# The opening of a one-core hybrid decoder kernel: first tile in halves, norm row by matmul, split first weights, a shorter inverse square root

## The chip, the cores and the metric

The kernel runs on one core of a Trainium2 chip. The core has five engines that run side by side: TensorE (PE, matrix products; its weight loads are shown as PEld), VectorE (DVE), ScalarE (ACT), GpSimd (POOL) and SyncE (SP, which here only issues transfers). Transfers between device memory and on-chip memory are carried out by 16 DMA engines, fed by SP and POOL. The metric is the device time of one execution in microseconds (us).

## The reference

One step of a hybrid layer. All of it reads the same normalised input; for the change, the norms matter:

```python
def rmsnorm(x, g):
    xf = x.astype(jnp.float32)
    y = xf * lax.rsqrt(jnp.mean(xf * xf, axis=-1, keepdims=True) + EPS)
    return (y * g.astype(jnp.float32)).astype(x.dtype)

def hybrid_layer(x, ...):
    hn = rmsnorm(x, g_norm)
    u = hn @ w_in                      # (1024, 7176)
    xa, za, uq, uk, uv, uo, zb, ui, uf = jnp.split(u, SPLIT_IDX, axis=-1)
    yA, hA, bufA = rglru_branch(xa, ...)
    hB, C, n, m = mlstm_seq(q, k, v, ig, lf, C0, n0, m0)
    yB = sigmoid(uo) * hB
    yB = yB * lax.rsqrt(jnp.mean(yB * yB, axis=-1, keepdims=True) + EPS) * g_mhead
    merged = concat([yA * silu(za), yB * silu(zb)])
    return x + merged @ w_out, ...
```

It is computed for a prompt of 1024 tokens and for 8 single sample tokens (with their states), and a last `rmsnorm` is put on the sum. Everything is float32.

## The kernel before, in words

**Precision and tiling.** A float32 operand is split into a high part (`A.copy` into the type fp32r, on ACT, L70) and a low part (`V.tensor_tensor` subtract, on DVE, L71). A product is then three matmuls (`mm3`, L64 to L66: high by high, high by low, low by high). Tokens are tiled by 128 rows, eight tiles `x0` to `x7`, and tile 8 holds the 8 sample tokens. `w_in` is read in units of 512 columns in two row halves (`raw0`, `raw1`), each column part `a` of 256 by its own transfer (`load_raw`, L214).

**The opening** (L468 to L503). TensorE has nothing to multiply yet and runs 17 products of a tile of ones with itself into `pw` (L468, "warming"). Meanwhile SP issues, in this order: the first token tile `x4` (L365, 512 KB), the norm gain `g_norm` written into all 128 rows of `gn_b` (L470, 512 KB written from a 4 KB row), the first weights `raw0` part 0 (L214, 512 KB), the gate weights `wg` (L472, 32 KB), `raw1` part 0, the second token tile `x0`, and parts 1 of `raw0` and `raw1`.

For each tile, `x_stats` sums the squares (ACT, L370, with a read of the accumulator) and takes the inverse root of the mean (`rsqrt_mean`, L180, then `rsqrt`, L184 to L188). `x_turn` multiplies by that number and by `gn_b` (DVE, L381; the first tile in two halves), and transposes on TensorE (L385). `x_split` makes high and low parts of the transposed tile (`b12h`, `b12l`, `cb_hi`, `cb_lo`), while `w0_split` and `w1_split` do so for the weights (`wph`, `wpl`; `w1h`, `w1l`). `plain` multiplies the tile by the first two column blocks (`wph`, then `w1h`), 24 products each, and stores them. `x_combos` forms sums of blocks that later products use. Token tiles and weight splits share six buffers (`ws`, NWS = 6): four hold `w1h` and `w1l`, so two remain for tiles of x, and the fetch of the third tile waits until the first has been transposed.

**After the opening** the units of `w_in` follow one another in seven products each; gates, the recurrent scan, decode steps and the chunked mLSTM are woven between them; at the end the output projection runs tile by tile, each with a final norm (`finish`, L1233), and the last tile's norm (`last_tile`, L1335 to L1340) stands at the very end.

**`rsqrt`** (L183 to L188) is called for the nine tiles of x, for each of the eight chunks of heads (`m_n`, four columns), once for the decode heads (32 columns), for the eight results of `finish` and in `last_tile`. It takes a root on ACT, a reciprocal on DVE, and one Newton step of three DVE instructions.

**What sets the order.** Each engine runs its own instructions in a fixed order. That order isn't the program's order throughout: the framework plans ahead from its own estimates of when data arrive and places an instruction where its inputs are expected. SP carries out its issues in order; an issue that waits for a buffer holds those behind it.

Of the kernel before, what the change touches and what calls it, by code (L numbers as in the profile page):

```python
# [9 lines left out]
F32 = mybir.dt.float32  # L10
F32R = mybir.dt.float32r
BF16 = mybir.dt.bfloat16
AF = mybir.ActivationFunctionType
ALU = mybir.AluOpType
# [3 lines left out]
P = 128  # L18
T = 1024
HT = 512  # L20
# [5 lines left out]
EPS = 1e-6  # L26
# [23 lines left out]
def hymba_kernel(  # L50
# [7 lines left out]
    V, A, G, TE = nc.vector, nc.scalar, nc.gpsimd, nc.tensor  # L58
    ld = nc.sync.dma_start
    stq = nc.gpsimd.dma_start  # L60

    def mm3(out, ah, al, bh, bl, first, last):

        TE.matmul(out, ah, bh, start=first, stop=False, skip_group_check=True)  # L64
        TE.matmul(out, ah, bl, start=False, stop=False, skip_group_check=True)  # L65
        TE.matmul(out, al, bh, start=False, stop=last, skip_group_check=True)  # L66
# [12 lines left out]
    def ps(tag, shape):  # L79
        return psp.tile(shape, F32, tag=tag, name=f"ps_{tag}", bufs=NBUF.get(tag, 1))  # L80
# [6 lines left out]
    rawp = ctx.enter_context(tc.tile_pool(name="rawp", bufs=1))  # L87
# [6 lines left out]
    def ws(shape, name, dt=F32R):  # L94

        return wsp.tile(shape, dt, tag="ws", name=name)

    def sg(shape, name, dt=F32):

        return stg.tile(shape, dt, tag="stg", name=name)  # L100
# [4 lines left out]
    def dconst(shape, name):  # L105

        return dpool.tile(shape, F32, tag=name, name=name)
# [4 lines left out]
    ones = dconst([P, P], "ones")  # L112
# [34 lines left out]
    st0 = dconst([P, 9, 3], "st0")  # L147
# [29 lines left out]

    def rsqrt_mean(out, v, t, n):

        V.tensor_scalar(v, v, 1.0 / n, EPS, op0=ALU.mult, op1=ALU.add)  # L180
        rsqrt(out, v, t)

    def rsqrt(out, v, t):  # L183
        A.activation(out, v, AF.Sqrt)  # L184
        V.reciprocal(out, out)
        V.tensor_tensor(t, out, out, op=ALU.mult)
        V.scalar_tensor_tensor(t, t, -0.5, v, op0=ALU.mult, op1=ALU.mult)
        V.scalar_tensor_tensor(out, t, 1.5, out, op0=ALU.add, op1=ALU.mult)  # L188

    cb = [(big(2 * q, [P, 4, HT], f"cb_hi{q}"), big(2 * q + 1, [P, 4, HT], f"cb_lo{q}")) for q in range(7)]  # L190

# [9 lines left out]
    COL = {"q": C_Q, "k": C_K, "v": C_V, "o": C_O, "z": C_ZB, "x": C_XA, "y": C_ZA}  # L201
    units = [((c[0], int(c[1])), (c[2], int(c[3]))) for c in UNITS]
    raws = {}

    def load_raw(u, b, parts=(0, 1)):

        if u >= len(units):
            return
        if (u, b) not in raws:
            raws[u, b] = rawp.tile([P, 4, 512], F32, tag=f"raw{b}", name=f"raw{b}_{u}")  # L210
        for a in parts:
            kind, j = units[u][a]
            c = COL[kind] + j * 256
            ld(raws[u, b][:, :, a * 256:(a + 1) * 256],  # L214
               w_in[0, b * HT:(b + 1) * HT, c:c + 256].rearrange("(k p) c -> p k c", p=P))
# [141 lines left out]
    fp = es_f.enter_context(tc.tile_pool(name="f_start", bufs=1))  # L357
    gn_b = fp.tile([P, T], F32, tag="gn_b", name="gn_b")
    xorder = [4, 0, 8, 5, 1, 6, 2, 7, 3]
    rows_of = lambda i: P if i < 8 else NB  # L360
    xt, xps, bf = {}, {}, {}

    def x_fetch(i):
        xt[i] = ws([P, T], f"x{i}", F32)
        ld(xt[i][:rows_of(i)], x_prompt[0, i * P:(i + 1) * P, :] if i < 8 else x_sample[:, 0, :])  # L365

    def x_stats(i):
        n = rows_of(i)
        junk = fp.tile([P, T], BF16, tag="junk", name="junk")
        A.activation(junk[:n], xt[i][:n], AF.Square, accum_out=st0[:n, i, 0:1])  # L370
        rsqrt_mean(st0[:n, i, 1:2], st0[:n, i, 0:1], st0[:n, i, 2:3], T)
# [92 lines left out]

    pw = ps("tr", [P, P])

    for _ in range(17):
        TE.matmul(pw, ones, ones, start=True, stop=True)  # L468
    x_fetch(xorder[0])
    ld(gn_b, g_norm[0].partition_broadcast(P))  # L470
    load_raw(0, 0, (0,))
    ld(wg, w_in[0, :, C_G:C_G + 8].rearrange("(k p) c -> p k c", p=P))  # L472
    load_raw(0, 1, (0,))
    x_fetch(xorder[1])
# [1 line left out]
    load_raw(0, 1, (1,))  # L476
    ld(bgate[:, 0:4], b_mi[0].partition_broadcast(P))
    ld(bgate[:, 4:8], b_mf[0].partition_broadcast(P))
    x_stats(xorder[0])
    x_stats(xorder[1])  # L480
    for m, i in enumerate(xorder):
        x_turn(m)
# [37 lines left out]
    fp = es_f.enter_context(tc.tile_pool(name="f_gates", bufs=1, reuse_waits="tile"))  # L520
# [414 lines left out]
    def decode_outputs():  # L935
# [36 lines left out]
        yield  # L972
        V.tensor_tensor(rsd, v4(tmp, 0), v4(tmp, 1), op=ALU.add)
        rsqrt_mean(rsq, rsd, rst, 4 * 256)
        V.tensor_tensor(num, num, dz, op=ALU.mult)
        V.tensor_tensor(num, num, gm4.unsqueeze(2).to_broadcast([P, 8, NB]), op=ALU.mult)
# [180 lines left out]
    def m_n(c):  # L1157

        m = ch[c]["m"]
        dn, ss, t, rs, u = (m[:, n] for n in range(5))  # L1160
        V.scalar_tensor_tensor(t, dn, -1.0, em_t[:, c, :], op0=ALU.mult, op1=ALU.max)
        V.tensor_tensor(t, t, dn, op=ALU.max)
        V.scalar_tensor_tensor(t, t, EPS, t, op0=ALU.mult, op1=ALU.mult)
        V.scalar_tensor_tensor(t, ss, 1.0 / (4 * 256), t, op0=ALU.mult, op1=ALU.add)
        rsqrt(rs, t, u)
        ch[c]["mh"], ch[c]["ml"] = ws([P, 8, P], f"mh{c}"), ws([P, 8, P], f"ml{c}")

# [64 lines left out]

    def finish(n, yt, ms, dst, later=False):  # L1233

        V.tensor_scalar(ms[:n, 0:1], ms[:n, 0:1], ms[:n, 1:2], 1.0 / T, op0=ALU.add, op1=ALU.mult)
        V.tensor_scalar(ms[:n, 0:1], ms[:n, 0:1], EPS, None, op0=ALU.add)
        rsqrt(ms[:n, 2:3], ms[:n, 0:1], ms[:n, 3:4])

        def out():
            for half in range(2):  # L1240
                hs = slice(half * HT, (half + 1) * HT)
                V.scalar_tensor_tensor(yt[half][:n], yt[half][:n], ms[:n, 2:3], mx["gf"][half][:n], op0=ALU.mult, op1=ALU.mult)
                stq(dst[:, hs], yt[half][:n])
        if later:
            tails.append(out)
        else:
            out()

    def dec_end():

        z = sg([P, HT], "zd")
        A.copy(z, dec_o[0])
        yd = [sg([32, HT], f"yd{half}") for half in range(2)]
        for half in range(2):
            stq(yd[half][0:NB], x_sample[:, 0, half * HT:(half + 1) * HT])
        yield
        ms = fms()
        for half in range(2):
            pd = ps("tr", [32, HT])
            TE.matmul(pd, sel[:, half, :], z, start=True, stop=True)  # L1260
            V.tensor_tensor(yd[half][0:NB], yd[half][0:NB], pd[0:NB], op=ALU.add)
            A.activation(pd[0:NB], yd[half][0:NB], AF.Square, accum_out=ms[0:NB, half:half + 1])
            yield
        finish(NB, yd, ms, y_s[:, 0, :])
# [50 lines left out]
    def last_tile():  # L1315
        x = ot[NCH - 1]
        ms = mx["p2"].tile([P, 6], F32, tag="ms7", name="ms7")
        y = [sg([P, HT], f"y{n}") for n in range(2)]
        yg = [sg([P, HT], f"yg{n}") for n in range(2)]
        for n in range(2):  # L1320
            stq(y[n], x_prompt[0, (NCH - 1) * P:T, n * HT:(n + 1) * HT])
        mh, ml = ch[NCH - 1]["mh"], ch[NCH - 1]["ml"]
        for i, cs in enumerate(LP):
            for k in range(8):
                w = wo[8 + k]
                mm3(x["p", i], mh[:, k, :], ml[:, k, :], w[:, 0, cs], w[:, 1, cs], False, k == 7)
            v = (y[0], y[1][:, 0:256], y[1][:, 256:512])[i]
            vg = (yg[0], yg[1][:, 0:256], yg[1][:, 256:512])[i]
            gv = (mx["gf"][0], mx["gf"][1][:, 0:256], mx["gf"][1][:, 256:512])[i]
            V.tensor_tensor(v, v, x["p", i], op=ALU.add)  # L1330
            A.activation(x["p", i], v, AF.Square, accum_out=ms[:, i:i + 1])
            V.tensor_tensor(vg, v, gv, op=ALU.mult)
            if i == 1:
                V.tensor_scalar(ms[:, 0:1], ms[:, 0:1], ms[:, 1:2], T * EPS, op0=ALU.add, op1=ALU.add)
        V.tensor_scalar(ms[:, 0:1], ms[:, 0:1], ms[:, 2:3], 1.0 / T, op0=ALU.add, op1=ALU.mult)  # L1335
        rsqrt(ms[:, 4:5], ms[:, 0:1], ms[:, 5:6])
        V.tensor_scalar(yg[0], yg[0], ms[:, 4:5], None, op0=ALU.mult)
        A.mul(yg[1], yg[1], ms[:, 4:5])
        for n in range(2):
            ld(y_p[0, (NCH - 1) * P:T, n * HT:(n + 1) * HT], yg[n])  # L1340
# [92 lines left out]
    for n in range(4, N):  # L1433
        c, h = n // 4, n % 4
# [8 lines left out]
        if h == 2 or n == 4:  # L1443
            z_load(c if h == 2 else 0)
        if h == 0:
            m_n(c - 1)
            fill(2)
            m_k(n + 1)
# [38 lines left out]
    while work:  # L1487
        fill(1)
    tail()
    last_tile()  # L1490
    es_m.close()

# [32 lines left out]
```

## Time and profile before

| what | value |
|---|---|
| runs (us) | 957.59, 960.5, 959.0; median 959.0 |
| the profiled execution's own time | 958.7 us |
| its span, first to last instruction | 956.9 us |
| mean granted TensorE clock | 0.997 of full speed |
| DVE, ACT, POOL busy | 75%, 61%, 15% of the span |

The profile gives times from the start of the span. "Idle before" an instruction is the time for which its engine had nothing to do, with what ended it. The chain that ended last is followed back from the last instruction: at each step to what released it. "PEclk" is the TensorE clock that was granted, as a share of full speed.

### The profile page before, as it was taken

How to read it: one execution, taken by the hardware profiler on the slowest of the kernel's cores; microseconds unless marked ns; L12 is line 12 of the kernel's file. 1: busy time of each engine (PE TensorE's matmuls, PEld its weight loads, DVE VectorE, ACT ScalarE, POOL GpSimd, SP SyncE). 2: the span in 40 equal slices, each digit the busy share in tenths (PEclk: the TensorE clock that was granted, in tenths of full speed). 3: DMA queues.
4: the chain of work that ended last, by engine and by line, in shares of the span. 5: the costliest groups of instructions: out<-in, count | busy, mean ns of one | idle time of the engine just before them, and what ended most of it. 6: DMA issues, size and time to landing. Idle time of an engine off the chain costs nothing.

```text
span 956.9 us, 15419 instructions
## 1 busy us (share of the span) xinstructions
PE 930.1 (97%) x5370; PEld 761.9 (80%) x5370; DVE 713.1 (75%) x1482; ACT 586.9 (61%) x1048; POOL 146.2 (15%) x259
## 2 busy tenths in 40 slices
PE   7999999999999999999899999999989999999997
PEld 7887767777787987777689898876667888888886
DVE  5876798879898878989687867686556676676664
ACT  5654447768677757677568774465546466455633
POOL 1111112112212122111211221010200100000020
PEclk9999999999999999999999999999999999999999
DMA  5441447356745465465537362434873763564361
GB/s 185 146 127 43 132 125 266 107 183 192 255 146 201 157 205 174 160 205 205 178 134 221 122 210 88 156 113 147 297 222 97 190 185 104 156 183 133 114 115 46
DMA packets 131363, 153.71 MB, mean 161 GB/s; under 512 B 15798, under 2 KB 110038, under 8 KB 131278
## 3 DMA queue, kind: packets, MB, share of 16 engines
q1 hardware_dynamic: 113558, 96.86, 34.5%
q0 software_dynamic: 17728, 55.87, 16.3%
q8 instruction: 42, 0.69, 0.3%
q14 instruction: 35, 0.29, 0.1%
HBM read 101.11 MB, written 51.65 MB: 160 GB/s over the span
## 4 chain that ended last, share of the span: by engine, by line
PE 71%; DVE 10%; DMA 8%; issue 5%; ACT 4%; SPq 1%; POOL 0%; DVEq 0%; ACTq 0%; POOLq 0%
PE ps_o L66 12%; PE ps_o L64 11%; PE ps_o L65 11%; PE ps_kv L64 8%; PE ps_kv L66 8%; PE ps_kv L65 8%; PE ps_tr L227 2%; DMA W<-d_alpha 2%; DMA Cb<-in_state_mlstm_C_dram 2%; PE ps_s L1075 1%; DMA out_dram<-Cb 1%; DVE wl L71 1%; DMA x<-in_x_prompt_dram 1%; PE ps_qp L64 1%; PE ps_tr L1211 1%
## 5 line engine op out<-in xcount | busy, mean ns | idle before, releaser
L64 PE MATMUL ps_kv<-cb_hi,wh 128*128 128x512 f32 x320 | 128.2, 401 | 3.5 <-ACT s L308 3.5
L71 DVE TENSOR_TENSOR wl<-raw,wh 128x1024 fp32r<-128x1024 f32 x91 | 111.2, 1222 | 27.2 <-ACT wh L70 16.8
L70 ACT CAST wh<-raw 128x1024 fp32r<-128x1024 f32 x91 | 95.4, 1048 | 58.3 <-PE ps_o L65 23.8
L66 PE MATMUL ps_kv<-cb_hi,wl 128*128 128x512 f32 x320 | 125.7, 393 | 0.0
L65 PE MATMUL ps_kv<-cb_lo,wh 128*128 128x512 f32 x320 | 125.2, 391 | 0.0
L64 PE MATMUL ps_o<-cb_hi,wh 128*128 128x512 f32 x240 | 95.0, 396 | 0.0
L66 PE MATMUL ps_o<-cb_hi,wl 128*128 128x512 f32 x240 | 94.1, 392 | 0.0
L65 PE MATMUL ps_o<-cb_lo,wh 128*128 128x512 f32 x240 | 93.5, 390 | 0.0
L64 PEld LDWEIGHTS ps_kv<-cb_hi,wh 128*128 128x128 f32 x320 | 60.1, 188 | 26.8 <-ACT s L308 4.5
L66 PEld LDWEIGHTS ps_kv<-cb_hi,wl 128*128 128x128 f32 x320 | 60.1, 188 | 15.6 <-issue 2.5
L65 PEld LDWEIGHTS ps_kv<-cb_lo,wh 128*128 128x128 f32 x320 | 60.2, 188 | 12.5 <-issue 0.8
L64 PE MATMUL ps_kv<-wh,cb_hi 128*128 128x256 f32 x192 | 55.4, 288 | 0.0
L65 PE MATMUL ps_kv<-wl,cb_hi 128*128 128x256 f32 x192 | 54.3, 283 | 0.0
L66 PE MATMUL ps_kv<-wh,cb_lo 128*128 128x256 f32 x192 | 54.3, 283 | 0.0
L64 PEld LDWEIGHTS ps_o<-cb_hi,wh 128*128 128x128 f32 x240 | 45.1, 188 | 10.7 <-issue 1.7
L66 PEld LDWEIGHTS ps_o<-cb_hi,wl 128*128 128x128 f32 x240 | 45.0, 188 | 10.6 <-issue 0.8
L64 PE MATMUL ps_o<-wo,rh 128*128 128x512 f32 (+1 forms) x136 | 53.4, 393 | 0.0
L66 PE MATMUL ps_o<-wo,ml 128*128 128x512 f32 (+1 forms) x136 | 52.1, 383 | 0.8 <-DVE ml L71 0.8
L64 PE MATMUL ps_o<-wo,mh 128*128 128x512 f32 (+1 forms) x136 | 52.8, 388 | 0.0
L65 PEld LDWEIGHTS ps_o<-cb_lo,wh 128*128 128x128 f32 x240 | 45.1, 188 | 9.2
L66 PE MATMUL ps_o<-wo,rl 128*128 128x512 f32 (+1 forms) x136 | 51.8, 381 | 0.0
L65 PE MATMUL ps_o<-wo,rh 128*128 128x512 f32 (+1 forms) x136 | 51.8, 381 | 0.0
(475 smaller groups left out, 2540.2 us busy)
## 6 DMA issues: line engine op xcount, KB each, us to landing
raw<-in_w_in_dram SPq DMA_DIRECT2D x56, 512.0 KB
Cb<-in_state_mlstm_C_dram SPq DMA_DIRECT2D x32, 256.0 KB
out_dram<-Cb POOLq DMA_DIRECT2D x32, 256.0 KB, 4.5
qk<-d_qk SPq DMA_DIRECT2D x32, 256.0 KB
oraw<-in_w_out_dram SPq DMA_DIRECT2D x16, 512.0 KB
d_qk<-s POOLq DMA_DIRECT2D x24, 256.0 KB, 4.4
x<-in_x_prompt_dram SPq DMA_DIRECT2D x8, 512.0 KB
d_x<-s POOLq DMA_DIRECT2D x16, 256.0 KB, 2.7
```

What stands on the lines that cost most here:

```text
L64: TE.matmul(out, ah, bh, start=first, stop=False, skip_group_check=True)
L65: TE.matmul(out, ah, bl, start=False, stop=False, skip_group_check=True)
L66: TE.matmul(out, al, bh, start=False, stop=last, skip_group_check=True)
L70: A.copy(hi, src)
L71: V.tensor_tensor(lo, src, hi.bitcast(F32), op=ALU.subtract)
L227: TE.matmul(pz[32 * g:32 * g + 32, :], hnd[:, k, :], raws[u, k // 4][:, k % 4, :], start=k < 4, stop=k >= 4, skip_group_check=True)
L1075: TE.matmul(S, qk[:, 2 + kb, :], qk[:, kb, :], start=kb == 0, stop=kb == 1)
L1211: TE.matmul(dec_o[0][32 * g:32 * g + 32, :], md, oraw[m][:, half * 512:(half + 1) * 512], start=n == 0, stop=n == 14, skip_group_check=True)
```

## The change

Four edits. In the opening, `x4` comes in two column halves of 256 KB, each squared and summed when it is there, and the two sums are combined on DVE (`x_first`, `x_first_stats`). `gn_b` isn't written by a transfer any more: two transfers of 2 KB bring the two halves of the row (`grow`), and two products of a column of ones with the row (one row deep, 512 columns) spread each over 128 rows in PSUM, which ACT copies to `gn_b`. They stand among the warming products, of which 6 + 3 remain out of 17. The first weights `raw0` part 0 come in two transfers of 256 KB. And `rsqrt` is written anew: with the mean scaled by a quarter, it is root, reciprocal, one step (multiply and add) and reciprocal where the operand is one column; for more columns that step takes two instructions.

```diff
     def rsqrt_mean(out, v, t, n):
-        V.tensor_scalar(v, v, 1.0 / n, EPS, op0=ALU.mult, op1=ALU.add)
+        V.tensor_scalar(v, v, 0.25 / n, 0.25 * EPS, op0=ALU.mult, op1=ALU.add)
         rsqrt(out, v, t)
     def rsqrt(out, v, t):
         A.activation(out, v, AF.Sqrt)
-        V.reciprocal(out, out)
-        V.tensor_tensor(t, out, out, op=ALU.mult)
-        V.scalar_tensor_tensor(t, t, -0.5, v, op0=ALU.mult, op1=ALU.mult)
-        V.scalar_tensor_tensor(out, t, 1.5, out, op0=ALU.add, op1=ALU.mult)
+        V.reciprocal(t, out)
+        if len(v.shape) == 2 and v.shape[1] == 1:
+            V.scalar_tensor_tensor(t, v, t, out, op0=ALU.mult, op1=ALU.add)
+        else:
+            V.tensor_tensor(t, t, v, op=ALU.mult)
+            V.tensor_tensor(t, t, out, op=ALU.add)
+        V.reciprocal(out, t)
...
+    def x_first():
+        i = xorder[0]
+        xt[i] = ws([P, T], f"x{i}", F32)
+        for half in range(2):
+            hs = slice(half * HT, (half + 1) * HT)
+            ld(xt[i][:, hs], x_prompt[0, i * P:(i + 1) * P, hs])
+
+    def x_first_stats():
+        i = xorder[0]
+        junk = fp.tile([P, T], BF16, tag="junk", name="junk")
+        sq = fp.tile([P, 2], F32, tag="sq", name="sq")
+        for half in range(2):
+            hs = slice(half * HT, (half + 1) * HT)
+            A.activation(junk[:, hs], xt[i][:, hs], AF.Square, accum_out=sq[:, half:half + 1])
+        v = st0[:, i, 0:1]
+        V.tensor_scalar(sq[:, 0:1], sq[:, 0:1], 0.25 / T, 0.25 * EPS, op0=ALU.mult, op1=ALU.add)
+        V.scalar_tensor_tensor(v, sq[:, 1:2], 0.25 / T, sq[:, 0:1], op0=ALU.mult, op1=ALU.add)
+        rsqrt(st0[:, i, 1:2], v, st0[:, i, 2:3])
...
     pw = ps("tr", [P, P])
-    for _ in range(17):
+    x_first()
+    grow = [sg([1, HT], f"grow{half}") for half in range(2)]
+    for half in range(2):
+        ld(grow[half], g_norm[:, half * HT:(half + 1) * HT])
+    raws[0, 0] = rawp.tile([P, 4, 512], F32, tag="raw0", name="raw0_0")
+    kind, j = units[0][0]
+    c0 = COL[kind] + j * 256
+    for k in (0, 2):
+        ld(raws[0, 0][:, k:k + 2, 0:256], w_in[0, k * P:(k + 2) * P, c0:c0 + 256].rearrange("(k p) c -> p k c", p=P))
+
+    for _ in range(6):
         TE.matmul(pw, ones, ones, start=True, stop=True)
-    x_fetch(xorder[0])
-    ld(gn_b, g_norm[0].partition_broadcast(P))
-    load_raw(0, 0, (0,))
+    for half in range(2):
+        pb = ps("o", [P, 512])
+        TE.matmul(pb, ones[0:1, :], grow[half], start=True, stop=True)
+        A.copy(gn_b[:, half * HT:(half + 1) * HT], pb)
+    for _ in range(3):
+        TE.matmul(pw, ones, ones, start=True, stop=True)
     ld(wg, w_in[0, :, C_G:C_G + 8].rearrange("(k p) c -> p k c", p=P))
...
-    x_stats(xorder[0])
+    x_first_stats()
     x_stats(xorder[1])
```

In `m_n`, `finish` and `last_tile` the constants in front of `rsqrt` are multiplied by 0.25, with the same instructions.

More of the change, by code (lines that the diff above doesn't have):

```diff
@@ L1162, in m_n @@
         V.tensor_tensor(t, t, dn, op=ALU.max)
-        V.scalar_tensor_tensor(t, t, EPS, t, op0=ALU.mult, op1=ALU.mult)
-        V.scalar_tensor_tensor(t, ss, 1.0 / (4 * 256), t, op0=ALU.mult, op1=ALU.add)
+        V.scalar_tensor_tensor(t, t, 0.25 * EPS, t, op0=ALU.mult, op1=ALU.mult)
+        V.scalar_tensor_tensor(t, ss, 0.25 / (4 * 256), t, op0=ALU.mult, op1=ALU.add)
         rsqrt(rs, t, u)
@@ L1233, in finish @@
     def finish(n, yt, ms, dst, later=False):
-        V.tensor_scalar(ms[:n, 0:1], ms[:n, 0:1], ms[:n, 1:2], 1.0 / T, op0=ALU.add, op1=ALU.mult)
-        V.tensor_scalar(ms[:n, 0:1], ms[:n, 0:1], EPS, None, op0=ALU.add)
+        V.tensor_scalar(ms[:n, 0:1], ms[:n, 0:1], ms[:n, 1:2], 0.25 / T, op0=ALU.add, op1=ALU.mult)
+        V.tensor_scalar(ms[:n, 0:1], ms[:n, 0:1], 0.25 * EPS, None, op0=ALU.add)
         rsqrt(ms[:n, 2:3], ms[:n, 0:1], ms[:n, 3:4])
@@ L1334, in last_tile @@
                 V.tensor_scalar(ms[:, 0:1], ms[:, 0:1], ms[:, 1:2], T * EPS, op0=ALU.add, op1=ALU.add)
-        V.tensor_scalar(ms[:, 0:1], ms[:, 0:1], ms[:, 2:3], 1.0 / T, op0=ALU.add, op1=ALU.mult)
+        V.tensor_scalar(ms[:, 0:1], ms[:, 0:1], ms[:, 2:3], 0.25 / T, op0=ALU.add, op1=ALU.mult)
         rsqrt(ms[:, 4:5], ms[:, 0:1], ms[:, 5:6])
```

## The prediction

> **What bounds the kernel now.** I read the page's span, shares and chain first.
>
> ```profile
> span 956.9 us, 15419 instructions
> PE 930.1 (97%) x5370; PEld 761.9 (80%) x5370; DVE 713.1 (75%) x1482; ACT 586.9 (61%) x1048; POOL 146.2 (15%) x259
> PE 71%; DVE 10%; DMA 8%; issue 5%; ACT 4%; SPq 1%; POOL 0%; DVEq 0%; ACTq 0%; POOLq 0%
> ```
>
> TensorE is busy all but 27 us, and the change touches none of its products after the opening. So only two things can be gained: an earlier start of the chain, and steps shorter where the chain runs over a norm. A start that comes earlier should pass on nearly whole, since everything later hangs on what came before and nothing is tied to an absolute time.
>
> So the timeline of the opening comes next.
>
> ```profile
> 1.14 6.53 PE L468 MATMUL ps_tr<-ones 128*128 128x128 f32 x34 [1.14 <-POOL ones L113]
> 4.53 1.06 ACT L370 ACTIVATE junk<-x 128x1024 bf16<-128x1024 f32 x1 [2.29 <-DMA x<-in_x_prompt_dram]
> 5.49 0.19 ACT L370 ACTIVATION_READ_ACCUMULATOR junk<-x 128x1 f32 x1
> 5.71 0.15 DVE L180 TENSOR_SCALAR st<-st 128x1 f32<-128x1 f32 x1 [5.71 <-ACT junk L370]
> 6.72 0.16 DVE L188 SCALAR_TENSOR_TENSOR st<-st 128x1 f32<-128x1 f32 x1
> 6.91 1.41 DVE L381 SCALAR_TENSOR_TENSOR x<-x,st,gn_b 128x512 f32<-128x512 f32 x2
> 7.76 1.27 PE L385 MATMUL ps_kv<-idF,x 128*128 128x128 f32 x8
> 8.05 0.62 ACT L70 CAST wph<-raw 128x512 fp32r<-128x512 f32 x1 [1.95 <-DMA raw<-in_w_in_dram]
> 8.57 0.24 ACT L70 CAST wph<-wg 128x64 fp32r<-128x64 f32 x1
> 8.72 0.61 ACT L70 CAST wph<-raw 128x512 fp32r<-128x512 f32 x1
> 9.24 0.57 ACT L70 CAST b12h<-ps_kv 128x512 fp32r<-128x512 f32 x1
> 10.92 0.39 PE L66 MATMUL ps_o<-wph,b12l 128*128 128x264 f32 x1 [0.55 <-DVE b12l L71]
> 11.23 0.59 ACT L407 COPY b12f<-ps_kv 128x512 f32<-128x512 f32 x1
> 14.53 1.07 ACT L70 CAST w1h<-raw 128x1024 fp32r<-128x1024 f32 x1
> 15.74 0.39 PE L65 MATMUL ps_o<-w1l,b12h 128*128 128x256 f32 x1 [0.92 <-DVE w1l L71]
> 17.48 1.28 DVE L381 SCALAR_TENSOR_TENSOR x<-x,st,gn_b 128x1024 f32<-128x1024 f32 x1
> 20.09 0.60 PE L385 MATMUL ps_s<-idF,x 128*128 128x128 f32 x4
> ```
>
> Two paths meet at the first useful product. Path one: `x4` lands (4.53), square, norm, scaling (6.91), transposes (7.76). Path two: the weights land only at 8.05; three casts then stand ahead of `b12h` on ACT, which starts at 9.24 though its first four transposes were through about 8.3. From 8.05 to the end of the cast at 15.6 ACT isn't idle at all. The chain agrees that the weights' transfer is the first long piece:
>
> ```profile
> 1.66 6.37 DMA raw<-in_w_in_dram
> 8.05 1.28 ACT wph L70 x3
> 21.16 3.89 DMA x<-in_x_prompt_dram
> 53.87 0.17 DVE st L186
> 54.07 0.17 DVE st L187
> 63.00 0.17 DVE st L188
> 952.29 0.17 DVE ms L187
> 952.48 0.17 DVE ms L188
> 952.68 0.72 ACT yg L1338
> ```
>
> It then runs over the second tile's transposes (20.09), the fetch of the next tile (21.16), and, further on, norms at 53.87, 63.0 and 952.3.
>
> **Part one: the norm row off the transfers.** It removes 512 KB that stand between `x4` and the first weights.
>
> ```profile
> 3.00:5.00 2.00, 2.00 (x11) 2.00 (x11) 0.00 (x0) 0.47 (x1) 0.00 (x0) 1.00 1.00 346
> 9.11 0.35 SPq L365 DMA_DIRECT2D x<-in_x_sample_dram  x1
> 1.66 0.43 SPq L214 DMA_DIRECT2D raw<-in_w_in_dram  x1
> ```
>
> The DMA engines are full, at 346 GB/s, so 524 kB are 1.5 us. The first weights would land at 8.05 - 1.5 = 6.5, and their first half another 262 / 346 = 0.76 us sooner, at 5.8. SP issues three transfers more in front of what follows (one half of x, one row half, one half of the weights: two of 0.43 and one of 0.35, 1.2 us). The weights' first issue moves from 1.66 to about 2.5, behind two issues of x and two of the row. I cost that at nothing: the 512 KB of x alone occupy the DMA engines until nearly 4, so the queue doesn't run empty. If it did, the loss would be at most that 0.8 us. The bounds for this part are -2.3 (the first half) and -0.7 (1.5 less 0.8) on the landing; for the later weights I take -1.5.
>
> Splitting x into halves is free by the same row: transfers behind each other overlap. A rule speaks against it. The Trainium skill, "DMA: Bandwidth & Descriptors", section "Bandwidth", asks for transfers of 1 MiB or more, because each carries a fixed cost of about 2 us. Paid in series it would put the second half of x 2 us later and my sum at about 959; the full DMA engines above say that it is overlapped.
>
> **Part two: the norm row by products.** It adds two products of 512 columns in float32, two copies on ACT, and removes eight warming products. A float32 matmul shows as two passes.
>
> ```profile
> 4.07 0.85 PE L468 MATMUL ps_tr<-ones 128*128 128x128 f32 x3
> 32.00 1.05 PE L227 MATMUL ps_tr<-raw,hnd 128*32 128x512 f32 x2
> ```
>
> Three passes of 128 columns start within 0.85 less the last one's 0.42, so 0.21 each; a product of 512 columns is 2 x 4 x 0.21 = 1.7 us at that early rate, and 1.05 us later, at full rate, by the row of 32.00. Six warming products end at 1.14 + 12 x 0.21 = 3.7. The row itself stands behind x in the queue; I let it land with x, at 4.5 (bounds: 3.7, when TensorE is free; 5.8, with the weights behind it). Product one then ends at 6.2, its copy (0.59, as the copy at 11.23) about 6.9. Product two ends at 7.3 at full rate or 7.9 at the early one, its copy at 7.9 or 8.5. The two copies fall where ACT is idle today (the 1.95 us ahead of 8.05); without that cover they cost 1.2.
>
> **Part three: halves of x and the shorter norm on path one.** The first half is squared while the second is under way, so after 4.53 only 512 columns are left: half of 1.06, saving about 0.5. `rsqrt` loses one DVE step of 0.2 (the spacing of 6.72 to 6.91). The factor would be ready at 6.91 - 0.5 - 0.2 = 6.2. But the scaling now waits for `gn_b`: first half at 6.9, exactly today's start; second half at 7.9 instead of 7.6. So path one gains nothing and its second half loses 0.3.
>
> **Part four: the meeting point.** With weights at 5.8 and 6.5, the three casts (8.05 to 9.24, 1.2 us) and the two copies fit on ACT between 5.8 and 8.2. `b12h` then starts when its transposes are through, 8.2 to 8.3, instead of 9.24: 1.0 us gained. After that ACT has the same 6.3 us of work in front of it as today, and the later weights come 1.5 us sooner, so the 1.0 us holds to `w1h` (14.53), the products at 15.74, the second tile's scaling and the fetch at 21.16. Bounds: the row late (5.8) puts scaling at 8.2 and `b12h` at 9.5, a loss of 0.3; the row early and the weights' whole 1.5 us bring -1.5.
>
> **Part five: the norms elsewhere.** One step of 0.2 falls away on the chain at 53.87 to 54.07 and at 63.0; in most other tiles it lies between splits that fill DVE. I take 0.4 (bounds 0.2 and 0.8: one tile pays, or four). At the very end nothing covers it: 0.2. In `m_n` and the decode heads the number of instructions is the same, four on DVE; cost nothing. The extra SP issues later: none.
>
> Sum: -1.0 - 0.4 - 0.2 = -1.6 us. The profiled execution took 958.7 us, 0.3 below the median of the three runs; 958.7 - 1.6 = **957.1 us**.
>
> **Rivals.**
>
> *The slow stretch goes too.* Windows of TensorE's clock:
>
> ```profile
> 9.76:13.17 3.41, 2.76 (x20) 2.55 (x21) 3.06 (x7) 3.41 (x8) 0.00 (x0) 1.00 1.06 346
> 13.17:16.58 3.41, 1.90 (x14) 1.50 (x13) 3.13 (x8) 2.95 (x6) 0.58 (x1) 1.00 0.22 60
> 16.58:20.00 3.42, 3.42 (x19) 3.42 (x18) 2.18 (x3) 0.00 (x0) 0.00 (x0) 0.50 0.02 5
> ```
>
> After a stretch with TensorE busy only 1.90 of 3.41 us the granted clock is 0.50 for 3.4 us. Were the products of `w1` at full rate, the second tile's transposes would start when its scaling ends, 17.48 + 1.28 = 18.8, not 20.09: another 1.2 us, 955.9. For it: 1.0 us earlier, more of the products at 15.74 fall into the window before 16.58. Against: the gap between the two blocks of products is the same length, since `w1h` moves with `wph`. The Trainium skill, "TensorE: Matmul & The Clock Gate", section "What's actually happening", says that this window runs freely and isn't tied to the kernel's start; by that rule the gap can fall across two windows in one execution and into one in another, before and after alike. The page's one execution can't show that.
>
> *The weights' lead is idle.* If `gn_b`'s second half and the DVE work behind it (scaling until 8.6, then the weights' low parts) hold `b12l` until today's time, the opening gains nothing: only the norms, -0.6, 958.1. For: the low part starts the stalled product at 10.92, not the high one. Against: the low parts of the weights can go before the scaling.
>
> *Slower: the copies stand ahead of the squares on ACT.* ACT runs in a planned order. If both copies are placed before the squares, they end at 7.9, the squares with their read at 9.1 instead of 5.7, 3.4 later; less 0.2 for the step, the scaling starts at 10.1 and `b12h` about 11.4, 2.2 later than 9.24. Norms give back 0.6: +1.6, 960.3. It decides from the point at which the planner expects the row before the second half of x. Against: the row is issued behind both halves.
>
> *The planned order differs further on.* If one fetch of a tile of x slips by a turn, it costs such a wait as the 3.89 at 21.16: 958.7 + 3.9 - 0.6 for the norms = 962.0. Nothing in the profile speaks for it.
>
> **How the numbers follow.** Forecast 0.38, slow stretch gone 0.28, lead idle 0.15, copies first 0.12, order 0.07. A measurement of this kernel tells a change from none at about 0.3%, 2.9 us: below 956.1 or above 961.9. Below lie 0.24 of the slow-stretch case and 0.15 of the forecast's (where the start gains 1.5 and the norms 0.8, 956.2 or less): 0.39. Above lie 0.03 of the copies-first case (row at 5.8, 1.3 later, and the second product at the early rate, 0.6 more: 962.2) and the order case: 0.10. Range: low 957.1 - 1.2 (slow stretch) - 0.9 (better bounds) = 955.0; high 960.3, the copies-first case.
>
> **What would show it.** Right: the first cast of weights near 5.8, `b12h` starting near 8.2, the first stalled product a microsecond before 10.92, the fetch of the third long tile near 20, three DVE steps after each root, and the last root's steps 0.2 shorter. Wrong: weights still landing near 8 (then the issue on SP held them); squares behind the copies; scaling well after 6.9; a clock of 1.00 throughout the opening would mean the second case. A difference after 70 us larger than at 21 would mean that the planned order changed.

## The result, and the profile after

The changed kernel is slower. Over 22 runs of each its median is 960.95 us against 956.76 us. The ratio is estimated as 1.0039 with a 95% interval of 1.0027 to 1.0051 (the quotient of the two medians alone is 1.0044): some 3.7 us lost where 1.6 us were forecast as gained.

The profiled execution of the changed kernel took 958.68 us. It is one of its quicker ones, 2.3 us under its median, so its page looks much like the page of before: the same span, TensorE as busy, and a chain with somewhat more of TensorE in it (79% against 71%). These are its span, its shares of busy time and the first line of its chain of waits.

```profile
span 956.9 us, 15387 instructions
PE 930.8 (97%) x5358; PEld 762.2 (80%) x5358; DVE 712.4 (74%) x1465; ACT 589.7 (62%) x1052; POOL 146.6 (15%) x259
PE 79%; DVE 8%; DMA 6%; ACT 3%; issue 3%; SPq 1%; POOL 0%; DVEq 0%; ACTq 0%; POOLq 0%
```

One pair of profiles can therefore show the steps, but not the whole loss. The timeline of the changed opening (start, duration, engine, line, operation; idle time before it in brackets):

```profile
1.14 2.93 PE L502 MATMUL ps_tr<-ones 128*128 128x128 f32 x12 [1.14 <-POOL ones L113]
3.86 1.49 PE L508 MATMUL ps_tr<-ones 128*128 128x128 f32 x6
5.28 2.25 PE L505 MATMUL ps_o<-grow,ones 1*128 1x512 f32 x4
5.68 0.16 DVE L192 RECIPROCAL st<-st 128x1 f32<-128x1 f32 x1
6.70 0.59 ACT L506 COPY gn_b<-ps_o 128x512 f32<-128x512 f32 x1 [1.50 <-PE ps_o L505]
7.18 0.62 ACT L70 CAST wph<-raw 128x512 fp32r<-128x512 f32 x1
7.32 0.75 DVE L405 SCALAR_TENSOR_TENSOR x<-x,st,gn_b 128x512 f32<-128x512 f32 x1 [1.47 <-ACT gn_b L506]
7.71 0.59 ACT L506 COPY gn_b<-ps_o 128x512 f32<-128x512 f32 x1
7.99 0.68 DVE L71 TENSOR_TENSOR wpl<-raw,wph 128x512 fp32r<-128x512 f32 x1
8.59 0.75 DVE L405 SCALAR_TENSOR_TENSOR x<-x,st,gn_b 128x512 f32<-128x512 f32 x1
8.89 0.59 ACT L70 CAST b12h<-ps_kv 128x512 fp32r<-128x512 f32 x1
9.39 1.12 PE L409 MATMUL ps_kv<-idF,x 128*128 128x128 f32 x4 [0.54 <-DVE x L405]
10.55 0.59 ACT L70 CAST cb_hi<-ps_kv 128x512 fp32r<-128x512 f32 x1 [1.07 <-PE ps_kv L409]
14.17 1.05 ACT L70 CAST w1h<-raw 128x1024 fp32r<-128x1024 f32 x1
16.50 1.28 DVE L405 SCALAR_TENSOR_TENSOR x<-x,st,gn_b 128x1024 f32<-128x1024 f32 x1
18.15 0.60 PE L409 MATMUL ps_s<-idF,x 128*128 128x128 f32 x4
```

The factor of the first tile is ready at 5.84, a microsecond sooner than before. But the scaling waits 1.47 us for the norm row, whose first product stands behind all nine warming products (12 + 6 passes), not between six and three. The planned order then puts a weights' cast (7.18) between the two copies on ACT, and a weights' low part (7.99) between the two scalings on DVE. The cast `b12h` starts 0.35 sooner than before; the one behind it, `cb_hi`, starts at 10.55. Before it was

```profile
9.71 0.59 ACT L70 CAST cb_hi<-ps_kv 128x512 fp32r<-128x512 f32 x1
13.33 1.06 ACT L70 CAST w1h<-raw 128x1024 fp32r<-128x1024 f32 x1
```

so the changed kernel is 0.84 late there, and the same 0.84 late at the first cast of the second weights (14.17). Not all of this is the late row: from 9.26 on TensorE runs at half rate, and the second four transposes take 1.12 us, where they take 0.66 at full rate (r1 below).

The second thing is the clock. Windows of the changed kernel (length, busy time of PE, PEld, DVE, ACT, POOL, then the granted clock, DMA share and GB/s):

```profile
2.44:5.85 3.41, 3.41 (x15) 3.11 (x15) 0.86 (x5) 1.59 (x5) 0.50 (x1) 1.00 0.93 273
5.85:9.26 3.41, 2.31 (x8) 0.79 (x6) 1.94 (x4) 2.56 (x6) 0.00 (x0) 1.00 1.06 306
9.26:12.68 3.42, 3.29 (x14) 3.06 (x15) 3.07 (x8) 2.35 (x6) 0.00 (x0) 0.50 1.03 329
```

TensorE is busy for 2.31 of 3.41 us from 5.85 on, 1.68 of it in the row products, and the clock falls to 0.50 for the next 3.42 us, in which the first useful products run. (The clock column shows 1.00 until the first change of the clock on record, here 5.85; in the opening before that, the spacing of products tells the rate, not the column. In the kernel before, passes of 128 columns start 0.21 us apart up to 6.2 us and 0.11 apart behind that.) In each profile the changes of the clock lie whole multiples of 3.41 us apart (here 5.85, 9.26, 12.68, 29.74); such a stretch is called a window here. Where the windows fall differs from one execution to the next: in the second profile of the changed kernel (a1 below) the clock rises at 4.20.

Over all runs the changed kernel's mean granted clock is 0.9907. The kernel before, over 17 to 31 runs beside each set of the experiments below, has 0.9938 to 0.9949. That is 0.0031 to 0.0042, or 6 to 8 us more at half rate in some 957 us; where TensorE is the bound, half of it, an estimate of 3 to 4 us, is lost. The loss measured is of that size. But this mean is a hint and no more. It leaves out the start before the first change: r3 below has 0.995 in its profile, although TensorE is at half rate until 17.16. And runs with a mean of 0.9917 and 0.9918 lose 1.4 us and nothing (r1 and w9 below).

### The profile page after: what moved, and what is told of

The parts are those of the page before. It is cut to its first block, busy times and chain, and to the rows that moved or that the text cites. A ratio compares the mean times of both kernels' runs of the same rounds, so it can differ in the third digit from the quotient of the medians.

```text
span 956.9 us, 15387 instructions
## 1 busy us (share of the span) xinstructions
PE 930.8 (97%) x5358; PEld 762.2 (80%) x5358; DVE 712.4 (74%) x1465; ACT 589.7 (62%) x1052; POOL 146.6 (15%) x259
## 4 chain that ended last, share of the span: by engine, by line
PE 79%; DVE 8%; DMA 6%; ACT 3%; issue 3%; SPq 1%; POOL 0%; DVEq 0%; ACTq 0%; POOLq 0%
PE ps_o L66 13%; PE ps_o L64 12%; PE ps_o L65 12%; PE ps_kv L64 9%; PE ps_kv L66 9%; PE ps_kv L65 9%; PE ps_tr L231 3%; DVE wl L71 1%; PE ps_s L1112 1%; DMA rh<-d_rm 1%; PE ps_qp L64 1%; PE ps_qp L946 1%; DMA Cb<-in_state_mlstm_C_dram 1%; PE ps_tr L1248 1%; PE ps_qp L65 1%
```

## The experiments

All ratios are against the kernel before, run on the same chip between them, and are estimated as the one above.

**Which half of the change loses.** The new `rsqrt` alone (opening as before), the new opening alone (`rsqrt` as before), and both kernels once more.

```diff
 # n1: kernel before, with the whole new rsqrt and the quarter constants
+        V.reciprocal(t, out)
...
+            V.scalar_tensor_tensor(t, v, t, out, op0=ALU.mult, op1=ALU.add)
...
+        V.reciprocal(out, t)
 # o1: changed kernel, with rsqrt and its constants as before
```

> The shorter inverse square root alone, with the quarter constants; opening as before. Theory A (the loss comes from the opening): 0.2 to 0.8 us faster than before, ratio 0.9992 to 0.9998, and the second tile's transposes earlier than 20. Theory B (the new root changes the planned order in the first 60 us and loses there): 2 to 4 us slower, ratio 1.002 to 1.004.

> The three edits of the opening alone, with the old inverse square root. Theory A: 3.5 to 5 us slower than before, ratio 1.0037 to 1.005, with a half-rate window of TensorE's clock in the first 14 us, after the wait for the norm row. Theory B: within 1 us of before.

> The kernel before, once more, as a measure of what two equal programs show. Both theories: ratio 1.000 within 0.0015. Its profile says whether the half-rate window at 16.6 to 20.0 is in every execution: theory A has it in some only.

> The changed kernel once more, for a second profile. Theory A: half-rate windows again in the first 14 us; if the half-rate windows at 29.7 and 698.8 are tied to the program they come again too, if they are chance they don't.

| run | ratio, 95% interval | mean clock of its runs |
|---|---|---|
| norms alone (n1) | 0.9989, 0.9976 to 1.0003 | 0.9937 |
| opening alone (o1) | 1.0024, 1.0009 to 1.0039 | 0.9928 |
| before again (b1) | 1.0000, 0.9987 to 1.0013 | 0.9949 |
| changed again (a1) | 1.0042, 1.0024 to 1.0059 | 0.990 |

The opening loses and the norms do not. The opening alone loses less than was expected of it (1.0037 or more). Multiplied, the two give 1.0013, against 1.0042 for the changed kernel on the same chip; with intervals of 0.0013 to 0.0018 each way this doesn't settle whether they also act on each other, and that stays open.

The profiles bear out the expected clock. In that of o1 TensorE is at half rate until 14.03. In the second one of the changed kernel (a1) the half rate comes again in the opening, from 7.62 to 11.03, and again behind it, from 28.10 to 34.93 and from 700.52 to 707.35. In that of b1 the half-rate window of 16.58 comes again, at 16.44.

The norms do more than was forecast. In the timeline of n1

```profile
14.34 0.16 DVE L192 RECIPROCAL st<-st 128x1 f32<-128x1 f32 x1
14.42 1.23 DVE L71 TENSOR_TENSOR w1l<-raw,w1h 128x1024 fp32r<-128x1024 f32 x1
15.56 1.28 DVE L385 SCALAR_TENSOR_TENSOR x<-x,st,gn_b 128x1024 f32<-128x1024 f32 x1
16.76 1.22 DVE L71 TENSOR_TENSOR w1l<-raw,w1h 128x1024 fp32r<-128x1024 f32 x1
17.23 0.60 PE L389 MATMUL ps_s<-idF,x 128*128 128x128 f32 x4
```

the second tile's scaling stands between the two weights' low parts; before, it came behind both, at 17.48. Nothing but the norms differs in n1, so it is their shorter chain of steps that moves it up in the planned order, and the transposes start 2.9 us sooner (17.23 against 20.09). The changed kernel has this too (16.50 and 18.15).

**Which part of the opening.** Three kernels: the changed one with the row in a zeroed tile of 128 rows, so that its products are 128 rows deep; the changed one with the norm row by its transfer; and the kernel before with nothing but the norm row by products.

```diff
 # r1: changed kernel, with
+    grow = [sg([P, HT], f"grow{half}") for half in range(2)]
+        V.memset(grow[half], 0.0)
+        ld(grow[half][0:1], g_norm[:, half * HT:(half + 1) * HT])
-        TE.matmul(pb, ones[0:1, :], grow[half], start=True, stop=True)
+        TE.matmul(pb, ones, grow[half], start=True, stop=True)
 # r2: changed kernel, 17 warming products, with
+    ld(gn_b, g_norm[0].partition_broadcast(P))
 # r3: kernel before, 6 + 3 warming products around
...
+        TE.matmul(pb, ones[0:1, :], grow[half], start=True, stop=True)
+        A.copy(gn_b[:, half * HT:(half + 1) * HT], pb)
```

> The changed kernel, but the row stands in a tile of 128 rows that is zero elsewhere, so that the two products that spread it are 128 rows deep instead of one; same length, same order, same result. Theory C (products one row deep leave TensorE's clock at half rate): no half-rate window in the first 16 us, mean granted clock 0.993 or more instead of 0.9907, and 1.5 to 3.5 us less than the changed kernel, ratio to before 0.9995 to 1.002. Theory D (the norm row's second half is late for the second half of the first tile, 0.84 us, and the clock has nothing to do with it): ratio stays at 1.003 to 1.005 and the clock at 0.991.

> The changed kernel without the row products: the norm row by its 512 KB transfer again, 17 warming products; x and first weights in halves, new inverse square root. Theories C and D both: the loss is gone, ratio 0.997 to 0.9995, clock 0.993 or more, no half-rate window before 12 us.

> The kernel before with only the norm row by two products one row deep (and 6 + 3 warming products); x and the first weights whole, old inverse square root. Theory C: it carries the loss by itself, ratio 1.0015 to 1.004, with a half-rate window or a late full rate in the first 14 us. Theory D: less than 0.001 slower, since the weights come later here and the copies lie ahead of them.

Without the row products (r2) the loss is gone: 0.9995, 0.998 to 1.0011, although in its profile the norm row landed only at 8.26 and `cb_hi` came at 10.78. With them alone (r3) it is there: 1.0031, 1.0012 to 1.005. With products 128 rows deep (r1) it is 1.0015, 0.9998 to 1.0031, between the two; and the mean clock of its runs, 0.9917, is lower than the 0.993 that theory C asked for. In the profiled execution of r3 TensorE ran at half rate up to 17.16, so the row products took 3.78 us instead of 2.25 and the second scaling came at 9.71:

```profile
5.28 3.78 PE L476 MATMUL ps_o<-grow,ones 1*128 1x512 f32 x4
9.09 0.59 ACT L477 COPY gn_b<-ps_o 128x512 f32<-128x512 f32 x1 [1.12 <-PE ps_o L476]
9.71 0.75 DVE L381 SCALAR_TENSOR_TENSOR x<-x,st,gn_b 128x512 f32<-128x512 f32 x1 [0.95 <-ACT gn_b L477]
11.67 0.59 ACT L70 CAST cb_hi<-ps_kv 128x512 fp32r<-128x512 f32 x1 [0.32 <-PE ps_kv L385]
```

Now r1, the same row products over 128 rows, in the window after the clock rose and the one behind it:

```profile
4.92:8.33 3.41, 2.62 (x10) 1.11 (x9) 2.30 (x7) 2.37 (x6) 0.00 (x0) 1.00 1.05 293
8.33:11.75 3.42, 2.37 (x18) 2.16 (x19) 3.42 (x8) 2.92 (x8) 0.00 (x0) 1.00 1.04 363
```

Busy for 2.62 of 3.41 us and then for 2.37 of 3.42 (a share of 0.69), r1 kept its clock until 28.81; the changed kernel, busy for 2.31 of 3.41 (0.68), lost it. What differs is that 1.68 of those 2.31 us were one row deep. The second profile of the changed kernel (a1) says it more plainly:

```profile
4.20:7.62 3.42, 2.72 (x12) 1.31 (x11) 1.89 (x7) 2.51 (x7) 0.00 (x0) 1.00 1.00 269
```

It was busy for longer than r1, 2.72 us, of which the row products took 1.98, and it lost its clock at 7.62. The share of busy time alone is not the rule: r1 kept full rate behind a window busy for 1.87 us (11.75 to 15.16) and lost it behind one busy for 2.17 (25.40 to 28.81).

And even at full rate the opening gains next to nothing (r1):

```profile
7.28 0.58 ACT L507 COPY gn_b<-ps_o 128x512 f32<-128x512 f32 x1
8.01 0.75 DVE L405 SCALAR_TENSOR_TENSOR x<-x,st,gn_b 128x512 f32<-128x512 f32 x1
8.81 0.66 PE L409 MATMUL ps_kv<-idF,x 128*128 128x128 f32 x4 [0.57 <-DVE x L405]
9.50 0.59 ACT L70 CAST cb_hi<-ps_kv 128x512 fp32r<-128x512 f32 x1 [0.50 <-PE ps_kv L409]
```

The second half of the norm row holds `cb_hi` until 9.50, 0.2 before 9.71. So both theories, the clock (C) and the late second half of the row (D), hold a part. But one or two executions of each, with other gaps in other places, do not prove that the depth of the products is what counts.

**The depth by itself.** In the kernel before, only the operands of the 17 warming products are cut to one row. No engine's planned order changes by one instruction. Beside it: the kernel before with 9 warming products, and r1 with products on the copied first half of the row, to keep TensorE busy behind the row products.

```diff
 # w1: kernel before, with
-        TE.matmul(pw, ones, ones, start=True, stop=True)
+        TE.matmul(pw, ones[0:1, :], ones[0:1, :], start=True, stop=True)
 # w9: kernel before, with
-    for _ in range(17):
+    for _ in range(9):
 # f1: r1, the last three warming products replaced, inside the loop over halves, by
+        if half == 0:
+            for _ in range(4):
+                TE.matmul(pw, ones, gn_b[:, 0:P], start=True, stop=True)
```

> The kernel before, with its 17 warming products one row deep instead of 128 (a row of ones with itself; their result is used by nobody). Number of instructions, planned order of every engine and busy time of TensorE stay the same. Theory C (products one row deep do not raise TensorE's clock): the granted clock stays at 0.50 through the first transposes and into the first 24 products, those products start 0.21 us apart instead of 0.12, the opening is longer by 1 to 2.5 us, ratio 1.001 to 1.003. Theory D (any busy TensorE raises the clock, the row products were only late): timeline and ratio as before, 0.999 to 1.001.

> The kernel before with 9 warming products instead of 17, nothing else; the norm row still comes by its transfer. TensorE is then idle from about 5 to 7.8 us. Theory E (the eight products removed carried the clock; the depth of the row products is a side matter): clock 0.50 in the first useful products, slower by 1 to 2.5 us, ratio 1.001 to 1.003. Theory C alone (only the row products hurt): ratio 0.999 to 1.001.

> The changed kernel with the norm row in a zeroed tile of 128 rows, products 128 rows deep, and in place of the last three warming products four products with the copied first half of the norm row, which fill TensorE between the row products and the transposes. If the clock was all (C): full rate from about 5 us through the opening, mean granted clock of the runs back at 0.994 or more, ratio 0.998 to 1.000 (norms -1.0, opening -0.2). If the late second half of the norm row (D) weighs: the cast cb_hi no earlier than 9.5, ratio 1.000 to 1.002 as with the 128-row products alone (1.0015).

The products one row deep (w1): 1.0016, 1.0005 to 1.0028, slower. Its timeline:

```profile
1.14 7.62 PE L468 MATMUL ps_tr<-ones 1*128 1x128 f32 x34 [1.14 <-POOL ones L113]
8.68 1.97 PE L385 MATMUL ps_kv<-idF,x 128*128 128x128 f32 x8
9.83 0.59 ACT L70 CAST b12h<-ps_kv 128x512 fp32r<-128x512 f32 x1 [0.47 <-PE ps_kv L385]
10.69 0.59 ACT L70 CAST cb_hi<-ps_kv 128x512 fp32r<-128x512 f32 x1 [0.27 <-PE ps_kv L385]
13.12 0.42 PE L65 MATMUL ps_o<-wpl,b12h 128*128 128x264 f32 x1
13.34 0.42 PE L66 MATMUL ps_o<-wph,b12l 128*128 128x264 f32 x1
```

and a window in the midst of its warming products:

```profile
4.03:7.44 3.41, 3.41 (x18) 3.41 (x17) 1.49 (x7) 1.35 (x3) 0.00 (x0) 1.00 1.00 317
```

TensorE is busy without a gap for 7.6 us, and still the transposes take 1.97 us instead of 1.27 and the useful products start 0.22 us apart as late as 13.3; the clock rises only at 14.27. In the kernel before the 34 passes took 6.53 us, because the clock rose in their midst. Nothing but the depth differs: products one row deep keep TensorE busy and do not raise its clock.

The ratio by itself would not rule out theory D, which allowed up to 1.001; the timeline does. Nor does the profile show how the slow opening becomes the loss at the end. Set against the kernel before, product by product (table below), w1 is about 1 us late in the opening, level at 18 to 20, where the kernel before is at half rate and w1 is not, and 1.1 late again behind a half-rate window of its own at 31.34.

With the row 128 deep and products behind it (f1) the loss is gone: 0.9987, 0.997 to 1.0003, the value of the norms alone, and clear of the changed kernel's interval. The opening then is worth nothing: `cb_hi` starts at 9.75. The mean clock of its runs, 0.9933, stays under the 0.994 that C asked for. f1 differs from the changed kernel in the depth and in the products behind, so its ratio can't tell these two apart; its windows can be set beside those of r3 (f1 first):

```profile
3.31:6.72 3.41, 3.19 (x7) 1.64 (x7) 0.86 (x5) 1.97 (x6) 0.00 (x0) 1.00 0.94 229
```

```profile
3.51:6.92 3.41, 3.41 (x11) 2.37 (x11) 0.79 (x5) 1.35 (x3) 0.00 (x0) 1.00 0.91 242
```

f1 was busy for 3.19 us, 2.44 of them in row products 128 rows deep, and its clock rose at 6.72. r3 was busy without a gap, but for the last 1.64 us with products one row deep, and its clock did not rise at 6.92.

The 9 warming products (w9) give no reading of their own: 0.9991, 0.9977 to 1.0006. In its profile TensorE is at half rate until 16.96, as theory E has it, and the mean clock of its runs is 0.9918. So the eight products taken out carried the clock too: with nine and no row products the opening can stay cold as well. But the shorter warming also moved the planned order: the second tile's scaling went ahead of both weights' low parts, to 14.25 instead of 17.48, and its transposes to 16.91. A slow opening and a sooner second tile work against each other, so the ratio doesn't price the slow opening.

**Products in the gap.** Three products more on each of two kernels, whose operand is the second column part of the first weights; they run in the first block of 24, just ahead of TensorE's gap between the two blocks.

```diff
 # g1, g2: n1, and h1: kernel before, with
             for b in range(2):
                 w1_split(b)
+            for k in range(3):
+                TE.matmul(pw, ones, raws[0, 0][:, k, 256:384], start=True, stop=True)
 # j1: f1 with the same three products;  n2: n1 again
```

> The kernel before with only the new inverse square root, and three more products with the second column part of the first weights, which keep TensorE busy just ahead of the gap between the two first blocks of 24. Candidate for the fastest: the norms alone measured 0.9989. If stretches at half rate cost what their length says and are brought on by idle gaps, there is none at 16 to 20 us and the mean granted clock is at least 0.0005 over that of the norms alone (0.9937): ratio 0.997 to 0.999. If the fillers only delay: 0.999 to 1.001.

> The kernel before with three products with the second column part of the first weights added in the first block of 24, and nothing else: every other instruction stands in the same planned order. If stretches at half rate, and not a new order, made the norms with these products the fastest (0.9957, the norms alone 0.9989): ratio 0.996 to 0.998, mean granted clock of the runs at 0.996 or more (before 0.9947), the products behind the gap start 0.12 us apart in its profile. If that result came with the norms in some other way: 0.999 to 1.001, as three products of 0.4 us that stand where TensorE waits anyway.

> The new inverse square root alone, once more. If the earlier 0.9989 holds: 0.998 to 1.000, mean granted clock near 0.9937.

> The norms with the three products, beside the norms alone on the same chip. If the three products take away later stretches at half rate: 0.995 to 0.997, mean granted clock 0.0015 or more above n2. If the first result was chance or the chip's: as n2, 0.998 to 1.000, the clocks within 0.001.

> The changed kernel with the row 128 deep, the four products behind it and the three products in the first block: all parts together. If the mended opening is worth its 0.2 us and the rest adds up: 0.0 to 0.4 us under g2, ratio 0.994 to 0.997; if the late second half of the norm row still weighs, 0 to 1 us over g2.

| run | ratio, 95% interval | mean clock of its runs |
|---|---|---|
| norms and three products (g1) | 0.9957, 0.9939 to 0.9974 | 0.9969 |
| the same again (g2) | 0.9957, 0.9944 to 0.9970 | 0.9954 |
| norms alone again (n2) | 0.9978, 0.9961 to 0.9996 | 0.9932 |
| three products alone (h1) | 0.9991, 0.9979 to 1.0003 | 0.9939 |
| all parts, opening mended (j1) | 0.9983, 0.9965 to 1.0001 | 0.9934 |

Norms and three products, 0.9957 on two chips, is the fastest version of all: 2.8 us under the norms alone by the medians on the same chip (g2 and n2), though their intervals overlap, and better than was expected of g1. The three products alone (h1) do what their second expectation said, next to nothing. All parts together (j1) miss both expectations, 3.0 us over g2 by the medians. What one slow window costs can be read between n1 and g2, whose planned orders differ by the three products only. The window from 28.83 on, n1 first, then g2:

```profile
28.83:32.24 3.41, 3.41 (x11) 1.42 (x9) 1.88 (x5) 3.21 (x7) 0.00 (x0) 0.50 0.64 209
```

```profile
28.83:32.24 3.41, 3.41 (x23) 2.40 (x22) 2.13 (x7) 3.09 (x7) 0.00 (x0) 1.00 0.62 201
```

11 matmuls against 23 in the same time. For every matmul of one kernel its start can be set against the start of the same matmul in another; the median of the differences, by the time in the run, is

| start at | 18 to 20 | 20 to 22 | 25 to 30 | 35 to 40 | 60 to 65 |
|---|---|---|---|---|---|
| changed less before | 0.74 | -1.94 | -2.22 | 0.26 | 0.13 |
| a1 (changed again) less before | -0.02 | -2.70 | -2.98 | 0.95 | 0.80 |
| n1 less before | -0.19 | -2.86 | -3.15 | -1.23 | -1.35 |
| g2 less before | -0.15 | -2.82 | -3.11 | -2.93 | -3.09 |
| o1 less before | 0.89 | 0.73 | 0.41 | 1.99 | 1.94 |
| r3 less before | 2.02 | 2.00 | 1.54 | 1.82 | 1.72 |
| w1 less before | -0.04 | -0.06 | -0.50 | 1.10 | 1.04 |

g2 keeps the norms' 3 us; n1 loses 1.7 of them in this one window. The changed kernel loses 2.5 there in one profile and 3.9 in the other (a1, at half rate from 28.10 to 34.93). Ahead of that, at 25 to 30, its opening has cost it 0.9 and 0.2 us, read against n1, which has the same norms. So most of what these two profiles show as lost by 40 us is not lost in the opening. r3, with no new norms, loses 2.0 in the opening and keeps most of that loss.

When TensorE first reached full rate in each profile, and its half-rate stretches from there up to 60 us (start and length):

| profile | full rate from | at half rate again |
|---|---|---|
| before, b1 | 6.34, 6.20 | 16.58 for 3.41; 16.44 for 3.41 |
| changed | 5.85 | 9.26 for 3.41, 29.74 for 3.41 |
| a1 (changed again) | 4.20 | 7.62 for 3.41, 28.10 for 6.83 |
| o1, r3, w1 | 14.03, 17.16, 14.27 | 31.10 for 3.41; none; 31.34 for 3.41 |
| w9 | 16.96 | 30.61 for 3.41 |
| r1, r2, f1 | 4.92, 6.30, 6.72 | 28.81 for 3.41; 30.20 for 3.41; 16.96 for 3.41 |
| n1 | 4.93 | 28.83 for 3.41 |
| n2 (n1 again) | 6.41 | 16.65 for 3.41, 30.30 for 3.41 |
| g1 | 4.47 | 11.30 for 3.41, 28.36 for 3.41 |
| g2 (g1 again) | 6.89 | none |
| h1 | 3.99 | 10.81 for 3.41, 31.30 for 3.41 |
| j1 | 4.47 | 11.30 for 3.41, 28.37 for 3.41 |

Between 8 and 14 us TensorE is at half rate at some time in all five profiles with products one row deep (changed, a1, o1, r3, w1), and in four of the other twelve (w9, g1, h1, j1). A half-rate stretch that begins between 28 and 31.4 stands in twelve of the seventeen, with and without such products; another, near 700 us, stands in all but that of the kernel before. So the row products bear on the clock of the opening, but the later windows, where the profiles lose more, are not theirs alone.

The mean clock is higher with norms and three products than with the norms alone in both sets, yet in the kernel before the same products raised nothing (h1, 0.9939 against 0.9944 for the runs beside it). Why products at 13 us help with the norms and not without them, and what they have to do with a window at 28.8, stays open: g1 and g2 are the same kernel, and one has that window and the other has not. By the medians j1 against g2 says that the opening, even mended, takes back some of what the norms and the products gain (their intervals still touch).

## Why the prediction was wrong

**The norm row by products (part two): the step that failed.** It priced the products by their length and the eight warming products taken out at nothing. The length was roughly right: 2.25 us in the changed kernel and 3.78 at half rate (r3), against 1.7 + 1.05 or 1.7 + 1.7. What was missing is the clock. A product one row deep keeps TensorE busy and does not raise its clock: w1 shows this with nothing else changed, and r3's full window shows it in place. In both profiles of the changed kernel the clock fell right where the useful products begin. With the row by its transfer (r2), or by deep products with others behind them (f1), the loss is gone; with the row products alone (r3) it is there.

Where a gain of 1.0 us was forecast, the opening cost 0.9 and 0.2 us at 25 to 30 in the two profiles of the changed kernel, and 1.5 in that of r3. That is less than the 3.7 us of the runs. By the profiles the rest goes in half-rate windows from 28 us on, which kernels without row products have too; whether and how the opening makes them cost more is not shown. Nor was taking out the eight warming products free: with nine of them and no row products (w9) the opening stayed at half rate until 16.96. I had a window row before me (1.90 busy of 3.41, then 0.50) and read it for the gap between two blocks only; I never asked what the opening's own windows would hold after the edit.

The Trainium skill, "TensorE: Matmul & The Clock Gate", section "What's actually happening", says that the clock follows how busy TensorE has been and rises after one busy window of some 3.4 us. Here 7.6 us of unbroken work one row deep did not raise it; the measurement decides.

**That an earlier start passes on nearly whole (the premise).** It was argued from nothing being tied to an absolute time. The clock's windows are: n1 is 3.15 us ahead at 25 to 30 and 1.23 at 35 to 40, behind one half-rate window.

**Where the row stands (also part two).** Forecast: products right behind six warming products, at 4.5. The planned order put all nine ahead, at 5.28. First scaling 7.32 (forecast 6.9), second 8.59 (forecast 7.9): the copies do not follow each other, a cast of weights stands between them, and a low part between the scalings. I had quoted that the order is planned, and then laid the instructions out in the program's order.

**The meeting point (part four).** `b12h` was forecast at 8.2 to 8.3 and came at 8.89. Worse, it was the wrong instruction to watch: the second cast, `cb_hi`, is next on ACT, hangs on the second half of the row, and came 0.84 later than before. The sentence that ACT has the same work in front of it after that was right, and so it carried the 0.84 on, of which some 0.46 are the second transposes at half rate (1.12 against 0.66). At full rate (r1) the gain there is 0.2, not 1.0; this bound, the rival of the idle lead, was nearer the truth than the forecast.

**The transfers (part one), and the halves (part three).** The factor was ready at 5.84 (forecast 6.2). Both savings are real and idle, since the row ends the wait. The second half of x was not 2 us behind the first: in r2, where ACT waits for both, the squares start at 3.50 and 4.42. r2, with halves, split weights and the new norms but no row products, is at 0.9995: without the row off the queue they gain nothing that shows.

**The norms (part five).** Forecast 0.6 us. By the ratios 0.9989 and 0.9978 they bring 1 to 2 us. The steps are shorter as forecast, but the largest gain that the profile shows comes from the planned order, 2.9 us at the second tile, and later windows take back a part of it.

**The rivals.** "The slow stretch goes too" came half true: the one at 16.58 is gone in the changed kernel's profile, and others stand at 9.26 and 29.74. That the windows fall otherwise in each execution, as this rival said, the two profiles of each of three kernels show (before, changed, the norms alone). No rival had the clock getting worse in the opening. The chance of 0.10 for slower came from two accidents of order; the clock was not among them.

## What to carry to other kernels

When work on TensorE is added, removed or reshaped near a stretch where the clock is just held, go through the clock's windows one by one and ask of each what will fill it, and with how many rows. Filler one row deep did not raise the clock here (w1); filler 128 rows deep did. One profile of each kernel is not enough for this, since the windows fall otherwise each time. Where a planner sets the order, a step saved or a product removed can move an instruction past another for more than the step is worth, so look at the new order before pricing anything behind it.

## What was not expected of the hardware

Products one row deep took as long as deep ones at half rate (passes 0.21 us apart in both) and did not raise the clock: 7.62 us of them without a gap, and the clock still rose only at 14.27 (w1). One window of 3.41 us at half rate cost 1.7 us where TensorE was the bound (n1 against g2).
